# Two transformer blocks in float32 on one core: first loads and gains from ScalarE's queue, another order of the opening products, zeros before two products

## The chip, the core and the metric

The kernel runs on one core of one Trainium2 chip. The metric is device time in microseconds (us) of one execution, and the median of several executions is taken. Before the change it is 1272.45 us, the median of 3 runs (1271.78 to 1274.7).

## The reference

The input x has 256 rows of 1024 columns, float32. Two layers run one after the other, each with three parts, and a last norm follows:

```python
for l in range(2):
    x = x + 0.5 * swiglu(rms_norm(x, ffn1_norm[l]), ffn1_w_gate[l], ffn1_w_up[l], ffn1_w_down[l])
    x = x + hybrid_mixer(rms_norm(x, mix_norm[l]), w_in[l], ...)
    x = x + 0.5 * swiglu(rms_norm(x, ffn2_norm[l]), ffn2_w_gate[l], ffn2_w_up[l], ffn2_w_down[l])
return rms_norm(x, final_norm)
```

`swiglu` multiplies by a gate and an up matrix of 1024 x 2816, forms silu(gate) * up, and multiplies by a down matrix of 2816 x 1024. `hybrid_mixer` has three kinds of attention, gates and an output matrix. All weights are float32, 247 MB are moved in all, and each weight is used once in an execution.

## The kernel before

**Products in three parts.** Each operand is split into a high and a low part. ScalarE writes the high part (`high`, L185), VectorE subtracts it to get the low part (`low`, L188), and TensorE adds up three matmuls (`mm3`, L176 to L178): high by high, low by high, high by low. So each piece of weights goes through four hands before TensorE can use it: a DMA into a raw place, ScalarE, VectorE, TensorE.

**Order.** The kernel writes out the instruction order of three engines itself: `ORDERED` (L61) names TensorE, ScalarE and VectorE, and they issue what they are given in the order in which the Python code emits it, DMA triggers on ScalarE included. SyncE (SP) and GpSimd (POOL) are ordered by a scheduler, which may put a load far ahead of its place in the program. The Python code keeps a clock of its own (`spend`, `defer`, `need`): `defer(us, fn)` emits work when TensorE's planned time has come that far.

**Loads.** `plan` and `plan_product` list the jobs in the order of use. `load` (L313) issues the DMA of a job, and emits the first step of its split at once and the others later. For a job without additions that first step is ScalarE's `high` of the whole job. The high and low parts lie in a ring of 6656 columns, so the splits run some jobs ahead of TensorE.

**A feed forward.** `first_block` (L574) multiplies two row tiles (t = 0, 1) by the first 256 columns of gate, then of up, k = 0 to 7 each. Two single blocks follow (`block`, g2 and u2). Then two units of seven products each for gate (G) and for up (U) come in the order 1, 5, 6, 3, 7, 2, 4, a Strassen scheme that needs sums of weight quarters: `steps` (L277) says for each product which quarter is loaded into which raw place (a with two buffers, b, c and d with one) and what is added by VectorE (L351) or by a POOL DMA (L331). Between the products stand blocks and down products: G1, D0, G5, g3, G6, u3, G3, D1, G7, D2, G2, g4, G4, u4, U1 and so on. So the raw places are filled for the first time by the loads for G1 (a), G5 (b), G6 (c), G2 (d) and U1 (the other a), each 768 KB, from L322.

**Norms.** `norm` (L405) makes one of these chains for the next part: square on ScalarE, root on VectorE and POOL, scale on VectorE (L450, L452), eight transposes on TensorE (`turn`), split (`parts_of`). The gains come by `gain_tile` (L208) on SP. The first norm has its gain by columns: `parts_of` multiplies (L471) and then splits. The opening (L1177 to L1196) loads x and the first weights, issues nine matmuls of zeros (L1186) and runs this norm for the first row tile; `second` (L1198) starts the second one, and `opened` (L1207) loads the tables `rot` and `tab` that the mixers use.

Of the kernel before, what the change touches and what calls it, by code (L numbers as in the profile page):

```python
# [13 lines left out]
ALU = mybir.AluOpType  # L14
AX = mybir.AxisListType

P = 128
# [93 lines left out]
def block_kernel(ctx: ExitStack, tc: tile.TileContext, a: dict, c: dict, out: bass.AP):  # L111
# [57 lines left out]
    def transpose(o, src, n=P):  # L169
        nc.tensor.transpose(o, src, ident[:n, :n])  # L170
        spend(0.11)

    def mm3(o, st, mv, first, last, again=False):

        (sh, sl), (mh, ml) = st, mv
        nc.tensor.matmul(o, sh, mh, start=first, stop=False, skip_group_check=again)  # L176
        nc.tensor.matmul(o, sl, mh, start=False, stop=False, skip_group_check=again)  # L177
        nc.tensor.matmul(o, sh, ml, start=False, stop=last, skip_group_check=again)  # L178
        spend(3 * (max(256, o.shape[-1]) / 2400 + 0.003))
        load_some()  # L180
        while later and later[0][0] <= clock[0]:
            heapq.heappop(later)[2]()
# [25 lines left out]
    def gain_tile(src, n, name, tag):  # L208

        g = small.tile([P, n], F32, tag=tag, name=name, bufs=1)  # L210
        nc.sync.dma_start(g, bass.AP(tensor=src.tensor, offset=src.offset, ap=[[0, P], [1, n]]))
        return g

    def x_in(t):
# [98 lines left out]
    def load(j, ring):  # L313
        job = jobs[j]
        name, n = job["name"], job["n"]
        adds = []
        if "unit" in job:
            places, new, add, source, more = job["unit"]
            if new:
                tag, src = new  # L320
                places[tag] = raw_place("raw" + tag, unit_pool[0], 2 if tag == "a" else 1, [P, 4 * UC], f"{name}_r", j)
                nc.sync.dma_start(places[tag][0].rearrange("p (k n) -> p k n", k=4), src)  # L322
            for t in {source, *(add or ()), *(more or ())[:1]}:
                for i in places[t][1]:
                    if i in loaded:
                        loaded[i][2]()
                if places[t][1][-1] != j:
                    places[t][1].append(j)
            if more:
                tag, src = more  # L330
                nc.gpsimd.dma_start(places[tag][0].rearrange("p (k n) -> p k n", k=4), src, accum_op=ALU.add)  # L331
            raw = places[source][0]
            if add:
                to, other = [places[t][0] for t in add]
                adds = [(to, other)]
        else:
            o, old = take(raws, n, j)
            for i in old:
                loaded[i][2]()
            raw = raws["tile"][:, o:o + n]  # L340
            o = 0
            for w, k0, k1, c0, m in job["runs"]:
                e = o + (k1 - k0) * m
                nc.sync.dma_start(raw[:, o:e].rearrange("p (k n) -> p k n", k=k1 - k0),
                                  w[k0 * P:k1 * P, c0:c0 + m].rearrange("(k p) n -> p k n", p=P))
                o = e
        o, _ = take(rings[ring], n, j)
        hi, lo = [rings[ring][i][:, o:o + n] for i in ("hi", "lo")]
        piece = n // 2 if adds else n if job["whole"] else PIECE
        cuts = [(o, min(n, o + piece)) for o in range(0, n, piece)]  # L350
        todo = [lambda o=o, e=e: nc.vector.tensor_tensor(to[:, o:e], to[:, o:e], other[:, o:e], op=ALU.add)  # L351
                for to, other in adds for o, e in cuts]
        todo += [lambda o=o, e=e: high(hi[:, o:e], raw[:, o:e]) for o, e in cuts]
        todo += [lambda o=o, e=e: low(lo[:, o:e], raw[:, o:e], hi[:, o:e]) for o, e in cuts]
        total = len(todo)

        def until(m):
            while len(todo) > m:
                todo.pop(0)()

        size = piece / 1200 + 0.1
        for m in range(total - 1, -1, -1):
            defer(size * (total - 1 - m), lambda m=m: until(m))
        until(total - 1)
        loaded[j] = hi, lo, lambda: until(0), ring
        return SUM if adds else SPLIT if "unit" in job else PACE * n
# [35 lines left out]
        tl = const.tile([P, KT, S], F32R, tag="xTl", name=f"{name}_Tl")  # L402
        return th, tl

    def norm(name, gain_src, last=None, gain_cols=None):  # L405


        st = {}

        def half_done(t, h):  # L410
            if "g" not in st:
                g = gain_cols is None and gain_tile(gain_src, D, f"{name}_g", "gain")
                st["g"] = g and [g[:, half_cols(i)] for i in range(2)]
                if last is None:
                    nT[name] = transposed(name)
            if h == 0:
                if last is not None:
                    st["xg", t] = row_tile(f"{name}_xg{t}")
                if last is not None and t == 0:
                    st["sq"] = row_tile(f"{name}_sq")  # L420
                st[t] = st["sq"] if last is not None else row_tile(f"{name}_xs{t}"), small.tile([P, 2], F32, tag="ss", name=f"{name}_ss{t}"), \
                    small.tile([P, 1], F32, tag="rstd", name=f"{name}_r{t}")
            defer(0.7, lambda: square(t, h))
            if last is not None:
                nc.vector.tensor_tensor(st["xg", t][:, half_cols(h)], x[t][:, half_cols(h)], st["g"][h], op=ALU.mult)
# [13 lines left out]
        def scaled(t):  # L439
# [8 lines left out]
            for h in range(2):  # L448
                if gain_cols is not None:
                    nc.vector.tensor_scalar(xs[:, half_cols(h)], x[t][:, half_cols(h)], r, None, op0=ALU.mult)  # L450
                else:
                    nc.vector.scalar_tensor_tensor(xs[:, half_cols(h)], x[t][:, half_cols(h)], r, st["g"][h], op0=ALU.mult, op1=ALU.mult)  # L452
                defer(0.8 + 0.7 * h, lambda h=h: turn(t, h))
            made.add((name, t, "rows"))

        def turn(t, h):
            tp = tp_bank(f"{name}_tp{t}{h}")
            for k in range(4):
                kk = h * 4 + k
                transpose(tp[:, k, :], st[t][0][:, kk * P:(kk + 1) * P])  # L460
            defer(0.3, lambda: parts_of(t, h, tp))

        def parts_of(t, h, tp):
            th, tl = nT[name]
            src = tp
            if name[0] == "f":
                if h == 0:
                    kept[name, t] = row_tile(f"{name}_xr{t}").rearrange("p (k s) -> p k s", s=P)
                if gain_cols is not None:
                    src = kept[name, t][:, h * 4:h * 4 + 4, :]  # L470
                    nc.vector.tensor_tensor(src, tp, gain_cols[:, h * 4:h * 4 + 4, None].to_broadcast([P, 4, P]), op=ALU.mult)  # L471
                    made.add((name, "kept", t, h))
            split(th[:, h * 4:h * 4 + 4, rows(t)], tl[:, h * 4:h * 4 + 4, rows(t)], src)
            if name[0] == "f" and gain_cols is None:
                defer(1.5, lambda: (nc.scalar.activation(kept[name, t][:, h * 4:h * 4 + 4, :], tp, AF.Copy), made.add((name, "kept", t, h))))
            made.add((name, t, h))
            if t == 1 and h == 1:
# [53 lines left out]
    def ffn(name, done, opening=None, opened=None):  # L531
        xTh, xTl = nT[name]
        steps, tail, f_first = ffn_steps()
        with ExitStack() as ctx2:
# [24 lines left out]
            def glu(g, u, nm, then, key):  # L559
# [11 lines left out]

                defer(0.25, silu)

            def first_block():  # L574

                pair = hidden(0, 2)
                for t in range(NT):
                    ab = acc_bank(f"{name}_b0{t}").rearrange("p (a b) -> p a b", a=2)
                    for i in range(2):
                        for k in range(KT):  # L580
                            need((name, t, k // 4))
                            mm3(ab[:, i, :], (xTh[:, k, rows(t)], xTl[:, k, rows(t)]), part(f"{name}_{'gu'[i]}0", k),
                                k == 0, k == KT - 1)
                        if opening and t == 0 and i == 0:
# [10 lines left out]
                                            made.update((name, "hT", i, t) for i in range(2))))  # L595

                    glu(ab[:, 0, :], ab[:, 1, :], f"{name}_b0{t}", lambda h, t=t: defer(2.5, lambda: turn(t, h)), (name, "h", 0, t))
                if opening:
                    opened()

            single = {}

# [120 lines left out]

            first_block()
            for step in steps:
                if step[0] == "P":
                    unit_product(*step[1:])
                elif step[0] == "B":
# [452 lines left out]
    nc.scalar.dma_start(gain_rows, a["ffn1_norm"][0].rearrange("(k p) -> k p", p=P))  # L1181
    nc.scalar.dma_start(ident, c["eye"])
    table(AF.Square)
    heat = acc_bank("heat")
    for _ in range(WARM):
        nc.tensor.matmul(heat[:, :256], zeros[:, :P], zeros, start=True, stop=True)  # L1186
    gain_bank = tp_bank("gain_tp")
    transpose(gain_bank[:, 0, :KT], gain_rows, KT)
    gain_cols = small.tile([P, KT], F32, tag="gc", name="gain_cols", bufs=1)
# [2 lines left out]
    first(0, 0)  # L1192
    first(0, 1)
    need(("f1_0", 0, "rows"))
    load(queues[0].pop(0), 0)
    need(("f1_0", 0, 0), ("f1_0", 0, 1))  # L1196

    def second():  # L1198
        x_in(1)
# [5 lines left out]
        pace[0] = clock[0]  # L1205

    def opened():  # L1207
        nc.sync.dma_start(rot, c["rot"])
        nc.sync.dma_start(tab, c["tab"])

    def write(t, h, rows_):
        (nc.scalar, nc.sync)[h].dma_start(out[0, rows(t), half_cols(h)], rows_[:, half_cols(h)])
# [2 lines left out]
    for i, (kind, l) in enumerate(layers):  # L1215
        if i + 1 < len(layers):
            k2, l2 = layers[i + 1]
            done = norm(f"{k2}_{l2}", a[norms[k2]][l2])
        else:
            done = norm("last", a["final_norm"], last=write)  # L1220
        if kind == "mx":
# [35 lines left out]
```

## Time and profile before

| | us |
|---|---|
| median of 3 runs | 1272.45 |
| the profiled execution's own time | 1275.12 |
| its span, first to last instruction | 1273.3 |
| TensorE busy in the span | 1254.1 |
| VectorE busy | 913.9 |
| ScalarE busy | 748.1 |

The profiled execution lies 2.67 us above the median. Times in the rows are counted from the start of the span. In a row of a timeline, the two numbers are the start and the duration in us, then come engine, line, operation, output<-inputs, shapes; in brackets stands how long the engine had been idle and what it waited for. PE is TensorE, DVE VectorE, ACT ScalarE; SPq and ACTq are DMA triggers.

### The profile page before, as it was taken

Reading aid. Unit: us, or ns where it says so; the run is one execution under the profiler, and the core shown is the slowest. Engines: PE = TensorE matmul, PEld = TensorE weight load, DVE = VectorE, ACT = ScalarE, POOL = GpSimd, SP = SyncE. Lnnn points to the kernel's source line nnn. Section 1 sums busy time; section 2 is a strip of 40 time slices with the busy share of each in tenths; the row PEclk is TensorE's granted clock in tenths of the full one; section 3 lists DMA queues with packets and bytes.
Section 4 is the critical chain, followed back from the end, with each engine's and each line's share of the span. In section 5 each row is a group of like instructions: output and inputs, shape, how many; then the busy total and the mean of one; then the engine's idle time right before and its main releaser. Section 6 shows DMA issues by size and latency. Waiting matters only on the chain.

```text
span 1273.3 us, 21204 instructions
## 1 busy us (share of the span) xinstructions
PE 1254.1 (98%) x8287; PEld 1178.7 (93%) x8287; DVE 913.9 (72%) x1359; ACT 748.1 (59%) x1263; POOL 55.6 (4%) x54
## 2 busy tenths in 40 slices
PE   7999999999999999999999999999999999999997
PEld 6999988999999899999889999899999998999996
DVE  5988767765546868887688877667655577788774
ACT  5665646655556456665466565467655554665652
POOL 0000001000000000000000000000000000000000
PEclk8999999999999999999999999999999999999999
DMA  9997856545435688986589985565464466799762
GB/s 301 259 263 207 225 189 172 153 131 145 127 111 169 208 256 221 267 229 174 165 261 261 247 239 151 168 178 154 134 165 115 135 198 199 215 267 242 221 167 79
DMA packets 206308, 247.28 MB, mean 194 GB/s; under 512 B 7160, under 2 KB 190208, under 8 KB 206208
## 3 DMA queue, kind: packets, MB, share of 16 engines
q1 hardware_dynamic: 188864, 220.16, 56.1%
q0 software_dynamic: 16896, 25.17, 12.1%
q8 instruction: 65, 1.06, 0.3%
q10 hardware_dynamic: 448, 0.59, 0.1%
q14 instruction: 35, 0.29, 0.1%
HBM read 244.85 MB, written 1.05 MB: 193 GB/s over the span
## 4 chain that ended last, share of the span: by engine, by line
PE 94%; DVE 3%; ACT 1%; DMA 1%; issue 0%; POOL 0%; POOLq 0%; ACTq 0%; DVEq 0%
PE f_a L178 6%; PE f_a L177 6%; PE f_a L176 6%; PE f_s L176 6%; PE f_s L177 6%; PE f_s L178 6%; PE f_b L177 6%; PE f_b L178 6%; PE f_b L176 6%; PE mx_ogate L176 4%; PE mx_ogate L178 3%; PE mx_ogate L177 3%; PE mx_odqk L176 2%; PE mx_odqk L177 2%; PE mx_odqk L178 2%; PE mx_sbdil L846 1%
## 5 line engine op out<-in xcount | busy, mean ns | idle before, releaser
L188 DVE TENSOR_TENSOR w_l<-w_r,w_h 128x512 fp32r<-128x512 f32 (+1 forms) x484 | 386.4, 824 | 96.7 <-ACT w_h L185 95.0
L185 ACT ACTIVATE w_h<-w_r 128x512 fp32r<-128x512 f32 (+1 forms) x484 | 344.3, 734 | 96.6 <-PE f_a L177 16.8
L176 PE MATMUL f_b<-f_Th,w_h 128*128 128x256 f32 x512 | 144.8, 283 | 0.0
L177 PE MATMUL f_b<-f_Th,w_l 128*128 128x256 f32 x512 | 144.6, 282 | 0.0
L178 PE MATMUL f_b<-f_Tl,w_h 128*128 128x256 f32 x512 | 144.6, 282 | 0.0
L178 PE MATMUL f_a<-w_l,f_hTh 128*128 128x512 f32 x352 | 139.8, 397 | 0.0
L176 PE MATMUL f_a<-w_h,f_hTh 128*128 128x512 f32 x352 | 139.1, 395 | 0.0
L177 PE MATMUL f_a<-w_h,f_hTl 128*128 128x512 f32 x352 | 138.7, 394 | 0.0
L188 DVE TENSOR_TENSOR w_l<-f_U_r,w_h 128x1536 fp32r<-128x1536 f32 (+1 forms) x72 | 100.2, 1399 | 33.1 <-ACT w_h L185 31.9
L185 ACT ACTIVATE w_h<-f_G_r 128x1536 fp32r<-128x1536 f32 (+1 forms) x72 | 86.2, 1199 | 46.4 <-DVE f_G_r L351 18.6
L176 PE MATMUL mx_ogate<-mx_Th,w_h 128*128 128x256 f32 x384 | 113.2, 295 | 0.0
L185 ACT ACTIVATE w_h<-f_U_r 128x1536 fp32r<-128x1536 f32 (+1 forms) x72 | 85.7, 1197 | 41.4 <-issue 14.1
L177 PE MATMUL mx_ogate<-mx_Th,w_l 128*128 128x256 f32 x384 | 108.7, 283 | 0.6 <-DVE w_l L188 0.6
L178 PE MATMUL mx_ogate<-mx_Tl,w_h 128*128 128x256 f32 x384 | 108.6, 283 | 0.0
L188 DVE TENSOR_TENSOR w_l<-f_G_r,w_h 128x1536 fp32r<-128x1536 f32 (+1 forms) x72 | 100.0, 1398 | 10.6 <-ACT w_h L185 10.2
L178 PEld LDWEIGHTS f_b<-f_Tl,w_h 128*128 128x128 f32 x512 | 97.9, 191 | 0.0
L177 PEld LDWEIGHTS f_b<-f_Th,w_l 128*128 128x128 f32 x512 | 97.7, 191 | 0.0
L176 PEld LDWEIGHTS f_b<-f_Th,w_h 128*128 128x128 f32 x512 | 97.6, 191 | 0.0
L176 PE MATMUL f_s<-w_h,f_Sh 128*128 128x384 f32 x256 | 87.3, 341 | 0.0
L178 PE MATMUL f_s<-w_l,f_Sh 128*128 128x384 f32 x256 | 86.7, 339 | 0.0
L177 PE MATMUL f_s<-w_h,f_Sl 128*128 128x384 f32 x256 | 86.6, 338 | 0.0
L178 PEld LDWEIGHTS f_a<-w_l,f_hTh 128*128 128x128 f32 x352 | 66.1, 188 | 15.7
(269 smaller groups left out, 2937.3 us busy)
## 6 DMA issues: line engine op xcount, KB each, us to landing
w_r<-in_ffn_w_down SPq DMA_DIRECT2D x88, 512.0 KB, 4.4
w_r<-in_w_in SPq DMA_DIRECT2D x84, 512.0 KB, 3.9
f_G_r<-in_ffn_w_gate SPq DMA_DIRECT2D x32, 768.0 KB, 7.7
f_U_r<-in_ffn_w_up SPq DMA_DIRECT2D x32, 768.0 KB, 8.6
w_r<-in_ffn_w_gate SPq DMA_DIRECT2D x40, 512.0 KB, 6.1
w_r<-in_ffn_w_up SPq DMA_DIRECT2D x40, 512.0 KB, 6.3
f_G_r<-in_ffn_w_gate POOLq DMA_DIRECT2D x16, 768.0 KB, 8.8
f_U_r<-in_ffn_w_up POOLq DMA_DIRECT2D x16, 768.0 KB, 8.4
```

The source lines that it names most:

```text
L176: nc.tensor.matmul(o, sh, mh, start=first, stop=False, skip_group_check=again)
L177: nc.tensor.matmul(o, sl, mh, start=False, stop=False, skip_group_check=again)
L178: nc.tensor.matmul(o, sh, ml, start=False, stop=last, skip_group_check=again)
L185: nc.scalar.activation(hi, src, AF.Copy)
L188: nc.vector.tensor_tensor(lo, src, hi.bitcast(F32), op=ALU.subtract)
L846: nc.tensor.matmul(o if len(k.shape) == 2 else o.rearrange("p (a b) -> p a b", a=NT), q, k, start=True, stop=True)
```

## The change

- `warm(n)` issues n matmuls of zeros. It is used with 9 at the start as before, with 3 ahead of the first product, and with 5 ahead of the second row tile's transposes in the norm that follows a second feed forward (that is between the two layers).
- Gains, `rot` and `tab` are loaded from ScalarE's queue. A norm's gain is emitted 40 planned us after the norm was set up, and `opened` is called before G4 of the first unit instead of after the first block.
- The first load into each raw place of the units (five loads in all) is issued from ScalarE's queue, the others from SP's as before.
- In the first norm, the multiplications by the gain and ScalarE's high parts come first, VectorE's low parts 1.2 planned us later; the second half's transposes follow 0.1 instead of 0.7 after the first's; the first weights' split is emitted 0.9 later.
- The first row tile's gate products go in two groups of four k: the four high by high, then the four low by high, then the four high by low (`by_parts`).

```diff
+    def warm(n):
+        heat = s_bank("heat")
+        for _ in range(n):
+            nc.tensor.matmul(heat[:, :256], zeros[:, :P], zeros, start=True, stop=True)
...
     def gain_tile(src, n, name, tag):
...
-        nc.sync.dma_start(g, bass.AP(tensor=src.tensor, offset=src.offset, ap=[[0, P], [1, n]]))
+        nc.scalar.dma_start(g, bass.AP(tensor=src.tensor, offset=src.offset, ap=[[0, P], [1, n]]))
...
                 places[tag] = raw_place("raw" + tag, unit_pool[0], 2 if tag == "a" else 1, [P, 4 * UC], f"{name}_r", j)
-                nc.sync.dma_start(places[tag][0].rearrange("p (k n) -> p k n", k=4), src)
+                first = len(users["raw" + tag]) <= (2 if tag == "a" else 1)
+                (nc.scalar if first else nc.sync).dma_start(places[tag][0].rearrange("p (k n) -> p k n", k=4), src)
...
-    def norm(name, gain_src, last=None, gain_cols=None):
+    def norm(name, gain_src, last=None, gain_cols=None, warmed=False):
...
+        if gain_cols is None:
+            defer(40.0, fetch)
...
-                defer(0.8 + 0.7 * h, lambda h=h: turn(t, h))
+                defer(0.8 + (0.7 if gain_cols is None else 0.1) * h, lambda h=h: turn(t, h))
...
         def turn(t, h):
+            if warmed and t == 1 and h == 0:
+                warm(5)
...
+            if gain_cols is not None:
+                src = kept[name, t][:, h * 4:h * 4 + 4, :]
+                nc.vector.tensor_tensor(src, tp, gain_cols[:, h * 4:h * 4 + 4, None].to_broadcast([P, 4, P]), op=ALU.mult)
+                made.add((name, "kept", t, h))
+                high(hi, src)
+                defer(1.2, lambda: (low(lo, src, hi), made.add((name, t, h))))
+                if t == 1 and h == 1:
+                    table(AF.Silu)
+                return
...
+            def by_parts(o, t, k0):
+                ks = range(k0, k0 + 4)
+                w = [part(f"{name}_g0", k) for k in ks]
+                for i, (a, b) in enumerate(((xTh, 0), (xTl, 0), (xTh, 1))):
+                    for k in ks:
+                        nc.tensor.matmul(o, a[:, k, rows(t)], w[k - k0][b], start=k == 0 and i == 0, stop=k == KT - 1 and i == 2)
+                spend(4 * 0.33)
...
+                            if opening and t == 0 and i == 0:
+                                if k % 4 == 0:
+                                    by_parts(ab[:, i, :], t, k)
+                                continue
...
-                if opening:
-                    opened()
...
+                if opening and step == ("P", 0, "G", 4):
+                    opened()
...
-    load(queues[0].pop(0), 0)
+    defer(0.9, lambda: load(queues[0].pop(0), 0))
     need(("f1_0", 0, 0), ("f1_0", 0, 1))
+    warm(3)
...
-        nc.sync.dma_start(rot, c["rot"])
-        nc.sync.dma_start(tab, c["tab"])
+        nc.scalar.dma_start(rot, c["rot"])
+        nc.scalar.dma_start(tab, c["tab"])
...
-            done = norm(f"{k2}_{l2}", a[norms[k2]][l2])
+            done = norm(f"{k2}_{l2}", a[norms[k2]][l2], warmed=kind == "f2")
```

## Rows read from the trace of the kernel before

**Rows 1.** The page, busy us (share of the span) x instructions.
```profile
PE 1254.1 (98%) x8287; PEld 1178.7 (93%) x8287; DVE 913.9 (72%) x1359; ACT 748.1 (59%) x1263; POOL 55.6 (4%) x54
```
**Rows 2.** Waits of TensorE in the whole span: us in total, times, longest.
```profile
PE f_tp L170 <- DVE f_xs L452: 1.8, 1, 1.8
...
PE mx_tp L170 <- DVE mx_xs L452: 0.8, 2, 0.4
```
**Rows 3.** Windows: length; busy us of PE, PEld, DVE, ACT, POOL; granted clock, DMA.
```profile
11.90:18.70 6.80, 5.71 (x24) 5.14 (x25) 5.43 (x11) 4.46 (x10) 0.55 (x1) 0.50 1.01 346
25.50:28.95 3.45, 3.40 (x16) 3.40 (x17) 2.75 (x5) 2.61 (x5) 0.00 (x0) 0.51 1.09 358
28.59:43.70 15.11, 15.11 (x111) 14.60 (x111) 15.03 (x22) 8.64 (x13) 1.45 (x1) 0.99 1.00 298
650.18:653.60 3.42, 3.42 (x19) 3.42 (x18) 2.43 (x3) 1.29 (x3) 0.00 (x0) 0.50 1.12 342
```
**Rows 4.** Timeline of the DMA triggers on SP in the opening.
```profile
6.50 1.35 SPq L322 DMA_DIRECT2D f_G_r<-in_ffn_w_gate  x1
...
14.95 0.38 SPq L344 DMA_DIRECT2D w_r<-in_ffn_w_gate  x1
```
**Rows 5.** Timeline of ScalarE in the first feed forward.
```profile
20.59 1.58 ACT L185 ACTIVATE w_h<-w_r 128x1024 fp32r<-128x1024 f32 x2 [3.23 <-DMA w_r<-in_ffn_w_gate]
...
29.32 1.49 ACT L185 ACTIVATE w_h<-f_G_r 128x1536 fp32r<-128x1536 f32 x1 [0.76 <-ACT f_f_b_s L564]
30.74 1.06 ACT L185 ACTIVATE w_h<-w_r 128x1024 fp32r<-128x1024 f32 x1
...
40.13 0.37 ACT L564 ACTIVATE f_f_b_s<-f_b 128x256 f32<-128x256 f32 x1
...
54.00 0.39 ACT L564 ACTIVATE f_f_b_s<-f_b 128x256 f32<-128x256 f32 x1 [1.30 <-PE f_b L178]
...
59.84 1.49 ACT L185 ACTIVATE w_h<-f_G_r 128x1536 fp32r<-128x1536 f32 x1 [1.81 <-issue]
```
**Rows 6.** Timeline of VectorE in the first feed forward.
```profile
13.57 0.69 DVE L188 TENSOR_TENSOR f_Tl<-f_xr,f_Th 128x512 fp32r<-128x512 f32 x1 [0.70 <-ACT f_Th L185]
14.18 1.89 DVE L188 TENSOR_TENSOR w_l<-w_r,w_h 128x512 fp32r<-128x512 f32 x3
...
30.98 1.75 DVE L188 TENSOR_TENSOR w_l<-f_G_r,w_h 128x1536 fp32r<-128x1536 f32 x1
...
34.72 0.95 DVE L351 TENSOR_TENSOR f_G_r<-f_G_r,f_G_r 128x768 f32<-128x768 f32 x1
...
42.40 0.95 DVE L351 TENSOR_TENSOR f_G_r<-f_G_r,f_G_r 128x768 f32<-128x768 f32 x1
...
45.38 1.95 DVE L188 TENSOR_TENSOR w_l<-f_G_r,w_h 128x768 fp32r<-128x768 f32 x2
...
56.70 1.76 DVE L188 TENSOR_TENSOR w_l<-f_G_r,w_h 128x1536 fp32r<-128x1536 f32 x1
...
65.16 1.76 DVE L188 TENSOR_TENSOR w_l<-f_U_r,w_h 128x1536 fp32r<-128x1536 f32 x1 [0.77 <-ACT w_h L185]
```
**Rows 7.** Timeline of TensorE: starts of the second row tile, G6, G2, U1.
```profile
24.83 0.38 PE L176 MATMUL f_b<-w_h,f_Th 128*128 128x256 f32 x1 [0.53 <-ACT f_Th L185]
...
48.81 0.34 PE L176 MATMUL f_s<-w_h,f_Sh 128*128 128x384 f32 x1
...
63.62 0.34 PE L176 MATMUL f_s<-w_h,f_Th 128*128 128x384 f32 x1
...
73.55 0.34 PE L176 MATMUL f_s<-w_h,f_Th 128*128 128x384 f32 x1
```
**Rows 8.** DMA issues (KB each, us to landing): one alone at 460.66; the fifth of five at 462.98.
```profile
f_G_r<-in_ffn_w_gate SPq DMA_DIRECT2D x1, 768.0 KB, 4.5
...
f_U_r<-in_ffn_w_up SPq DMA_DIRECT2D x1, 768.0 KB, 10.6
```
**Rows 9.** TensorE by groups between 5.1 and 7.2 us: busy, mean ns.
```profile
L1186 PE MATMUL heat<-zeros 128*128 128x256 f32 x10 | 2.5, 393 | 0.0
```

More of the change, by code (lines that the diff above doesn't have):

```diff
@@ L403, in transposed, with fetch @@
         return th, tl
-    def norm(name, gain_src, last=None, gain_cols=None):
+    def norm(name, gain_src, last=None, gain_cols=None, warmed=False):
         st = {}
+        def fetch():
+            if "g" not in st:
+                g = gain_tile(gain_src, D, f"{name}_g", "gain")
+                st["g"] = [g[:, half_cols(i)] for i in range(2)]
+        if gain_cols is None:
+            defer(40.0, fetch)
         def half_done(t, h):
-            if "g" not in st:
-                g = gain_cols is None and gain_tile(gain_src, D, f"{name}_g", "gain")
-                st["g"] = g and [g[:, half_cols(i)] for i in range(2)]
+            if "begun" not in st:
+                st["begun"] = True
+                if gain_cols is None:
+                    fetch()
                 if last is None:
@@ L464, in parts_of @@
             th, tl = nT[name]
-            src = tp
-            if name[0] == "f":
[L467 to L474, printed above, removed]
+            hi, lo = [o[:, h * 4:h * 4 + 4, rows(t)] for o in (th, tl)]
+            if name[0] == "f" and h == 0:
+                kept[name, t] = row_tile(f"{name}_xr{t}").rearrange("p (k s) -> p k s", s=P)
+            if gain_cols is not None:
[7 more added lines that the diff above has]
+                return
+            split(hi, lo, tp)
+            if name[0] == "f":
                 defer(1.5, lambda: (nc.scalar.activation(kept[name, t][:, h * 4:h * 4 + 4, :], tp, AF.Copy), made.add((name, "kept", t, h))))
@@ L1183, in block_kernel @@
     table(AF.Square)
-    heat = acc_bank("heat")
-    for _ in range(WARM):
-        nc.tensor.matmul(heat[:, :256], zeros[:, :P], zeros, start=True, stop=True)
+    warm(WARM)
     gain_bank = tp_bank("gain_tp")
```

## The prediction

> **What bounds the kernel now.** The page's busy times come first: TensorE works through 98% of the span, the other engines through 72% and less [rows 1], so the kernel is bound by TensorE, and a change can only win where TensorE stands still or runs at its lower clock. The list of TensorE's waits says where that is: nearly everything lies in the first 26 us, one gap of 1.8 us lies between the two layers, and two gaps of 0.4 us lie at the mixers' starts [rows 2]. [...] From 28.59 to 43.7 us VectorE is busy for 15.03 of 15.11 us while TensorE never waits [rows 3]: the splits of the first unit's weights are only just ahead of their use. G6's low part is made in two pieces from 45.38 on, the first done by 46.35 (half of 1.95 us), and TensorE begins G6 at 48.81 [rows 6, 7]: a lead of 2.45 us. It is the smallest lead of the unit; G2 has 63.62 - 58.46 = 5.2 us and U1 73.55 - 66.92 = 6.6 us [rows 6, 7].
>
> **The opening.** TensorE reaches the second row tile at 24.83 [rows 7]. Following the chain back: ScalarE stood for 3.23 us at the weights of g2, which landed just before 20.59 [rows 5], because SP could issue them only at 14.95 [rows 4], when VectorE had finished the low part of the first weights and so cleared their raw place [rows 6]. In that low part's queue VectorE waited 0.70 us for ScalarE, and so it did once more before it [rows 6]. With the new order (both gain products, then the low parts) the six VectorE steps of 0.6 to 0.7 us follow each other without those two waits, and the place is clear near 13.5: 1.4 us earlier. G1's 768 KB and the tables no longer stand on SP ahead of g2 [rows 4]; without them I take 4.5 us for landing instead of 5.6 [rows 8]. So g2 lands near 17.9, 2.7 us earlier, and the chain behind it (high parts, low parts, the second tile's gain products) comes along: second tile at 22.1. The bounds of this are 1.4 (the DMA is no quicker) and 4.4 us (the half clock of 25.5 to 28.95, worth 3.45 / 2 = 1.7, goes too).
>
> The products by parts and the three zeros have no term of their own: TensorE finishes the first tile's products sooner, but then waits for g2's chain. Nine zeros stay as they were. Three matmuls of zeros are six passes of 0.21 us and lie in the wait for the first high part.
>
> **The five loads.** This is the term that decides. In the before, SP issued G1's load at 6.50 [rows 4], 23 us before ScalarE used it at 29.32 without waiting for data [rows 5]. On ScalarE's queue the trigger stands in the written order, and `load` emits the high part directly behind the DMA. So ScalarE triggers, and waits for the landing, with all that is queued behind it: the next weights' high parts, silu, the splits of hidden values; VectorE then waits for ScalarE. What a landing costs, L, is bounded by two rows: a load of this size alone took 4.5 us, the fifth of five issued within 2.3 us took 10.6 [rows 8], which is 4.5 plus some 2.1 for each one ahead less the time between the issues. I take 4.5, since SP runs dry while the splits stand still.
>
> [...]
>
> Step by step, times in the trace's own span:
> - G1: ScalarE is free at 29.32 - 0.76 = 28.56 in the before [rows 5]; less 2.7, and 0.4 for the low parts that now follow, 25.5. Landing at 30.0, high part to 31.5 (1.49), so VectorE's low part starts at 31.5 instead of 30.98 [rows 6]: +0.5, though TensorE is 2.7 earlier. G1 itself is not late.
> - G5: VectorE adds the quarter from raw place b at 34.72 [rows 6]. Its trigger stands behind G1's high part, D0's (1.06), a split and a silu (0.37 each) [rows 5]: 33.3, landing 37.8. +3.1.
> - G6: in the before its trigger's place is behind the silu at 40.13 to 40.50 [rows 5], 5.8 us after G5's addition: 37.8 + 5.8 = 43.6, landing 48.1 instead of an addition at 42.40 [rows 6]. +5.7. Less the lead of 2.45, TensorE begins G6 **3.2 us later** than before. The whole gain of the opening is used up on the way: VectorE sets this time.
> - G2: VectorE recovers 1 of ScalarE's 1.3 us of idle time at 54.00 [rows 5] (5.7 - 1.0 = 4.7 behind), then 4.5 for the landing: 9.2 behind, less the lead 5.2 and the 3.2 that TensorE has lost: **+0.8**.
> - U1: 9.2 behind, less 1.8 idle at 59.84 [rows 5] and 1.1 at shorter waits, plus 0.9 for the triggers of `rot` and `tab` (0.38 each at best [rows 4]), plus 4.5: 11.7, less the lead 6.6 and the 4.0 lost: **+1.1**.
>
> Sum of the first feed forward: +5.1. Every us of L counts five times (three at G6, one each at G2 and U1). From U5 on the loads are SP's again and run ahead as before.
>
> **Zeros between the layers.** TensorE's gap ends with the norm's scale, so zeros cannot shorten it. Five matmuls are ten passes; ten took 2.5 us at the opening's full clock with the ends of the first and last counted [rows 9], some 2.1 back to back, 0.3 more than the gap [rows 2]. If the clock stays up, the 3.42 us at half clock behind it, in which TensorE never waited [rows 3], give back 1.7. **-1.4**, between +0.3 (the clock falls anyway) and -1.7.
>
> **Gains from ScalarE.** q_norm's and kv_norm's triggers stand at each mixer's start, just ahead of the squares on which the waits of 0.4 us hang [rows 2]. Two triggers of 0.4 to 0.5 us, less the idle time in which they fall: +0.3 each, **+0.6**; bounds 0 and 2. The norms' gains are emitted in mid-stage, where ScalarE has idle time (59% busy [rows 1]); uncovered they would cost 0.4 us each.
>
> **Sum:** +5.1 - 1.4 + 0.6 = +4.3. Against the profiled execution, 1275.12 + 4.3 = 1279.4; that execution stands 2.67 above the median, so in medians 1272.45 + 4.3 = **1276.7 us**. Some 0.2% (2.5 us) is what a measurement of this kernel can tell from no change.
>
> **Rivals.**
> - *The loads are covered* (faster). If ScalarE's five triggers stand far enough ahead of their use, or land within 3.4 us, G6's lead holds, and the opening's 2.7, with part of the 1.7 of the clock, reaches the end: -3.3 - 1.4 + 0.6 = -4.1, **1268.3**. It decides at 3L = 10.2, or L = 3.4: below that TensorE meets G6 no later than before. For it: a scheduler put SP's G1 load 23 us ahead [rows 4, 5]. Against it: ScalarE is one of the three engines whose order is written out, and a load of this size took 4.5 us with nothing ahead of it [rows 8]. [...]
> - *Partly covered.* With L at 3.8 in effect (ScalarE somewhat earlier at its triggers than I put it), 5 x 0.7 = 3.5 us less: 1276.7 - 3.5 = **1273.2**, not to be told from no change.
> - *Shared bandwidth.* SP's loads of g3, u3 and D1 are in flight beside ScalarE's; L = 5.5: +5.0, **1281.7**.
> - *Zeros do nothing*: the clock falls between the layers all the same, +1.7: **1278.4**. This would be the part of the change that does not do what it is said to.
>
> **How the numbers follow.** The serial landings, with the last two rivals as their variants, 0.55: slower. Covered, 0.25: faster. Partly covered, 0.20: same. The forecast's own range is 1274 to 1282; the other cases pull the lower end to the covered case's 1268.3, the upper end to L of nearly 6: 1268 to 1283.
>
> **What would show it.** Right: ScalarE idles over 3 us before L185 on f_G_r, released by a DMA that it triggered itself just before; VectorE idles before L351; TensorE waits, where it never did, before G6 near 50 us, and may show a lower clock behind it; the second row tile starts near 22; no window of half clock after 650. Wrong: landings of ScalarE's loads that end before their high part is due, TensorE busy without a break from 30 to 75 us, or a first feed forward that ends earlier than before.

## The result, and the profile after

The changed kernel takes 1289.42 us (median of 4 runs, 1287.93 to 1292.18) against 1273.56 us of the kernel before in the same series: ratio 1.0131, 95% interval 1.0118 to 1.0144. It is 15.9 us slower. The prediction had the sign and the reason, but 1276.7 us and a range that ended at 1283. The profiled execution took 1288.44 us, its span is 1286.7 us.

The longest of TensorE's waits in the whole span (us in total, times, longest), in answer to [rows 2]:

```profile
PE f_s L182 <- ACT w_h L191: 4.1, 1, 4.1
PE f_b0tp L170 <- DVE f_f_b_h L590: 3.9, 1, 3.9
PE f_s L182 <- DVE f_G_g L717: 2.5, 1, 2.5
```

All three are new: ahead of G2, ahead of the transposes of the second row tile's first hidden values, and ahead of U1. The wait of 1.8 us between the layers is gone; a stretch of zeros stands there.

TensorE's timeline at the start of the second row tile and of G6, and where it waited, in answer to [rows 7]:

```profile
21.50 0.38 PE L182 MATMUL f_b<-w_h,f_Th 128*128 128x256 f32 x1 [0.52 <-ACT f_Th L191]
...
36.89 0.69 PE L170 MATMUL f_b0tp<-ident,f_f_b_h 128*128 128x128 f32 x2 [3.88 <-DVE f_f_b_h L590]
...
51.53 0.34 PE L182 MATMUL f_s<-w_h,f_Sh 128*128 128x384 f32 x1
...
70.58 0.69 PE L182 MATMUL f_s<-w_h,f_Th 128*128 128x384 f32 x1 [4.08 <-ACT w_h L191]
...
86.52 0.49 PE L182 MATMUL f_s<-w_h,f_Th 128*128 128x384 f32 x1 [2.48 <-DVE f_G_g L717]
```

Against [rows 7] the second tile starts 3.3 us earlier (24.83 to 21.50), G6 2.7 us later (48.81 to 51.53), G2 7.0 us later (63.62 to 70.58) and U1 13.0 us later (73.55 to 86.52). From there to the end little is added, since 1.7 us of half clock behind U1 and 1.4 us gained between the layers nearly cancel: the spans differ by 13.4 us. All of the loss lies between 21 and 90 us.

ScalarE's timeline shows the cause, in answer to [rows 5] (a row with ACTq is a DMA trigger):

```profile
21.43 0.39 ACTq L329 DMA_DIRECT2D f_G_r<-in_ffn_w_gate  x1
...
24.42 0.36 ACT L586 ACTIVATE f_f_b_s<-f_b 128x256 f32<-128x256 f32 x1
29.68 1.49 ACT L191 ACTIVATE w_h<-f_G_r 128x1536 fp32r<-128x1536 f32 x1 [4.90 <-DMA f_G_r<-in_ffn_w_gate]
29.88 0.39 ACTq L329 DMA_DIRECT2D f_G_r<-in_ffn_w_gate  x1
31.08 1.04 ACT L191 ACTIVATE w_h<-w_r 128x1024 fp32r<-128x1024 f32 x1
32.02 0.36 ACT L191 ACTIVATE f_hTh<-f_b0tp 128x256 fp32r<-128x256 f32 x1
32.29 0.38 ACT L586 ACTIVATE f_f_b_s<-f_b 128x256 f32<-128x256 f32 x1
...
59.59 0.38 ACTq L329 DMA_DIRECT2D f_G_r<-in_ffn_w_gate  x1
69.05 1.48 ACT L191 ACTIVATE w_h<-f_G_r 128x1536 fp32r<-128x1536 f32 x1 [9.04 <-DMA f_G_r<-in_ffn_w_gate]
...
73.96 0.37 ACTq L329 DMA_DIRECT2D f_U_r<-in_ffn_w_up  x1
...
82.64 1.48 ACT L191 ACTIVATE w_h<-f_U_r 128x1536 fp32r<-128x1536 f32 x1 [8.01 <-DMA f_U_r<-in_ffn_w_up]
```

ScalarE stands 4.9, 9.04 and 8.01 us at loads that it triggered itself just before, those of G1, G2 and U1. Behind G1's high part stand D0's (31.08), the split of the first tile's hidden values (32.02) and silu of the second tile (32.29). VectorE stands the same way, behind ScalarE at G1, at G6's quarter, and behind ScalarE at G2 and U1:

```profile
31.20 1.76 DVE L194 TENSOR_TENSOR w_l<-f_G_r,w_h 128x1536 fp32r<-128x1536 f32 x1 [3.04 <-ACT w_h L191]
...
34.95 0.95 DVE L358 TENSOR_TENSOR f_G_r<-f_G_r,f_G_r 128x768 f32<-128x768 f32 x1
...
36.42 0.41 DVE L590 TENSOR_TENSOR f_f_b_h<-f_f_b_s,f_b 128x256 f32<-128x256 f32 x1
...
47.22 0.96 DVE L358 TENSOR_TENSOR f_G_r<-f_G_r,f_G_r 128x768 f32<-128x768 f32 x1 [4.51 <-DMA f_G_r<-in_ffn_w_gate]
...
70.56 1.76 DVE L194 TENSOR_TENSOR w_l<-f_G_r,w_h 128x1536 fp32r<-128x1536 f32 x1 [9.63 <-ACT w_h L191]
...
84.16 1.76 DVE L194 TENSOR_TENSOR w_l<-f_U_r,w_h 128x1536 fp32r<-128x1536 f32 x1 [7.43 <-ACT w_h L191]
```

The hidden values of the second tile (36.42) are what TensorE waits 3.88 us for at 36.89. Their silu had ended at 32.67; what held them was VectorE, which works without a break from G1's low part at 31.20 on. In the kernel before they came at nearly the same time, but TensorE came for them only at 37.66, 1.06 us after they were done:

```profile
36.19 0.41 DVE L568 TENSOR_TENSOR f_f_b_h<-f_f_b_s,f_b 128x256 f32<-128x256 f32 x1
```

```profile
37.66 0.38 PE L170 MATMUL f_b0tp<-ident,f_f_b_h 128*128 128x128 f32 x2
```

The landings of the five loads, from the list of DMA issues (KB each, us from trigger to landing), in the order G1, G5, G6, G2, U1:

```profile
f_G_r<-in_ffn_w_gate ACTq DMA_DIRECT2D x1, 768.0 KB, 8.1
...
f_G_r<-in_ffn_w_gate ACTq DMA_DIRECT2D x1, 768.0 KB, 4.5
...
f_G_r<-in_ffn_w_gate ACTq DMA_DIRECT2D x1, 768.0 KB, 7.5
...
f_G_r<-in_ffn_w_gate ACTq DMA_DIRECT2D x1, 768.0 KB, 9.4
...
f_U_r<-in_ffn_w_up ACTq DMA_DIRECT2D x1, 768.0 KB, 8.6
```

Only G5's takes the 4.5 us of a load alone [rows 8]. Last, the windows at half clock, in answer to [rows 3]:

```profile
35.51:42.33 6.82, 5.44 (x21) 5.44 (x22) 6.82 (x11) 3.89 (x7) 1.45 (x1) 0.50 0.38 100
...
69.64:76.47 6.83, 5.10 (x16) 4.60 (x17) 5.91 (x5) 4.99 (x6) 0.00 (x0) 0.50 0.58 162
86.71:90.12 3.41, 3.41 (x12) 3.41 (x12) 3.29 (x4) 1.85 (x4) 0.28 (x1) 0.50 0.64 198
```

Each lies behind or around one of the new waits; none is left in the opening or between the layers. TensorE works 13.95 us in them, which by the granted clock of 0.50 costs at most half, an estimate of 7.0 us; in the profile of before it was 5.71 + 3.40 + 3.42, half of it 6.3 us. There 128x256 matmuls start every 0.21 us at 0.50 (652.0 on) and every 0.12 at 1.00 (653.8 on). So the clock has moved to other places and is no large part of the difference by itself.

### The profile page after: what moved, and what is told of

It reads as the page before. It is cut to its first block, busy times and chain, and to the rows that moved or that the text cites. A ratio compares the mean times of both kernels' runs of the same rounds, so it can differ in the third digit from the quotient of the medians.

```text
span 1286.7 us, 21240 instructions
## 1 busy us (share of the span) xinstructions
PE 1259.0 (98%) x8303; PEld 1182.1 (92%) x8303; DVE 913.1 (71%) x1359; ACT 746.8 (58%) x1263; POOL 55.6 (4%) x54
## 3 DMA queue, kind: packets, MB, share of 16 engines
q1 hardware_dynamic: 184496, 211.71, 53.4%
q8 instruction: 65, 1.06, 0.3%
## 4 chain that ended last, share of the span: by engine, by line
PE 91%; DVE 3%; DMA 3%; ACT 1%; issue 1%; POOL 0%; POOLq 0%; ACTq 0%; DVEq 0%
PE f_a L184 6%; PE f_a L183 6%; PE f_a L182 6%; PE f_s L182 6%; PE f_s L183 6%; PE f_s L184 6%; PE f_b L182 5%; PE f_b L183 5%; PE f_b L184 5%; PE mx_ogate L182 4%; PE mx_ogate L183 4%; PE mx_ogate L184 4%; DMA f_G_r<-in_ffn_w_gate 2%; PE mx_odqk L182 2%; PE mx_odqk L183 2%; PE mx_odqk L184 2%
```

## The experiments

**The five loads back on SP (e1_sp).** One line of the changed kernel:

```diff
-                first = len(users["raw" + tag]) <= (2 if tag == "a" else 1)
+                first = False
```

> The changed kernel with the five first loads (G1, G5, G6, G2, U1) back on SP's queue and nothing else undone. Theory: the five loads carry the whole loss, the opening gains 4.8 us (first tile stage ends at 26.88 instead of 31.69) and the zeros between the layers 1.0, and these reach the end once TensorE no longer waits for the units: about 1267.8 us, 5 to 6 under the kernel before, no wait of TensorE over 1 us between 30 and 90 us. Rival: the moved table and gain triggers or the new order of the opening cost as well: the time stays above 1276.

Measured: 1272.84 us, ratio to before 0.9999 (0.9990 to 1.0008). The whole loss is gone, so it was the five loads'; but none of the expected gain is there either. The first two of them now start on SP ahead of g2, and ScalarE's next step shows it:

```profile
6.43 2.96 SPq L329 DMA_DIRECT2D f_G_r<-in_ffn_w_gate  x2
13.20 0.37 SPq L351 DMA_DIRECT2D w_r<-in_ffn_w_gate  x1
...
20.26 1.57 ACT L191 ACTIVATE w_h<-w_r 128x1024 fp32r<-128x1024 f32 x2 [4.22 <-DMA w_r<-in_ffn_w_gate]
```

g2's load, triggered at 13.20, takes 7.0 us (5.6 in the kernel before, 3.9 in the changed one). What the new order gains at the trigger (14.95 to 13.20) the landing gives back, and the second row tile starts at 24.49. So the opening's gain needs an emptier queue ahead of g2 (7.0 us behind two unit loads, 3.9 behind none), which the same move had bought.

**The five loads alone (e2_only).** The kernel before with the lines on `first` and nothing else.

> The kernel before with the five first loads on ScalarE's queue and nothing else. Theory: the loss is theirs alone, and without the earlier opening TensorE loses about as much: 14 to 19 us over the kernel before (1287 to 1292), waits before G2 and U1, the half clock behind them. Rival: the loss comes from the loads together with the new order of the opening (a wait that falls where the first tile ends 4.8 us earlier): at most 5 us over the kernel before.

Measured: 1289.33 us, ratio 1.0134 (1.0108 to 1.0159), 16.4 us over before. TensorE waits 6.6 us at the second tile's first hidden values, 4.0 ahead of G2 and 2.7 ahead of U1. The rest of the change neither makes the loss nor softens it beyond the noise. This run also has no unit load ahead of g2, but the old order of the opening. g2's load is triggered at 15.21 and takes 4.2 us; the second row tile starts between before (24.83) and after (21.50):

```profile
23.63 0.38 PE L176 MATMUL f_b<-w_h,f_Th 128*128 128x256 f32 x1 [0.52 <-ACT f_Th L185]
```

So the new order alone (e1_sp) brings 0.3 us there, the emptier queue alone 1.2, both together 3.3. The starts of these runs differ by up to 0.4 us.

**Which loads cost how much (e6_gu).** G2's and U1's first loads on SP, the other three on ScalarE:

```diff
-                first = len(users["raw" + tag]) <= (2 if tag == "a" else 1)
+                first = len(users["raw" + tag]) <= 1 and tag != "d"
```

> The changed kernel with G2's and U1's first loads on SP, and G1's, G5's and G6's left on ScalarE. Theory: of the 15.9 us, G2 and U1 with the half clock behind their two waits carry most (TensorE falls from +2.6 to +14.6 us between 48 and 90 us): 1276 to 1279. Rival: the delay already stands in ScalarE's and VectorE's queues when G6 has been split and G2 would be late whoever loads it: 1284 or more.

Measured: 1279.38 us, ratio 1.0049 (1.0035 to 1.0064), just above the theory's span and far below the rival's. Against the changed kernel some 10 us are G2's and U1's; against e1_sp 6.5 us are left for G1, G5 and G6.

**The same queue, triggered early (e3_early).** All five triggers on ScalarE's queue, but together behind u2's high part.

```diff
+        if name.startswith("f1_0_u2"):
+            fetch_units()
```

> The changed kernel with the same five loads on the same queue, ScalarE's, but all five triggers emitted together right behind the high part of u2, ahead of the first silu. Theory: the place of the trigger, right ahead of its own high part, is what costs; the queue itself does not: about 1268 us (5 to 6 under the kernel before), G2's and U1's landing long before their high parts. Rival: ScalarE's queue is served badly beside SP's and POOL's, wherever the trigger stands: over 1280, ScalarE still waiting for G2's or U1's load.

Measured: 1273.74 us, ratio 1.0009 (1.0000 to 1.0018): 15.7 us better than in the written places, so the place of the trigger is what costs. But it is not the expected 1268. ScalarE's timeline:

```profile
22.14 0.95 ACTq L325 DMA_DIRECT2D f_G_r<-in_ffn_w_gate  x2
...
26.40 3.65 ACTq L325 DMA_DIRECT2D f_U_r<-in_ffn_w_up  x1
30.09 0.38 ACT L598 ACTIVATE f_f_b_s<-f_b 128x256 f32<-128x256 f32 x1 [4.87 <-issue]
```

The five triggers take 7.9 us from the first to the end of the last (22.14 to 30.05), the last alone 3.65, and silu of the first tile stands behind them for 4.87 us. The wait has only changed its name: ScalarE now stands at issuing instead of at the landing, and TensorE waits 3.2 us behind it, with 6.8 us at half clock around the wait (a mean granted clock of 0.66 from 30 to 40 us).

**One load ahead of g2, none in ScalarE's order (e12_one).** All five on SP, but VectorE writes one column of four of the places late in its order, so that only G1's load can start ahead of g2:

```diff
+    def gate():
+        for tag in "bcd":
+            gated[tag] = raw_place("raw" + tag, unit_pool[0], 1, [P, 4 * UC], f"gated_{tag}", None)
+            nc.vector.tensor_copy(gated[tag][0][:, :1], x[1][:, :1])
...
+                places[tag] = gated.pop(tag) if tag in gated else raw_place(...)
...
+                first = False
...
+                if tag == "a" and len(users["rawa"]) == 1:
+                    gated[tag] = raw_place("rawa", unit_pool[0], 2, [P, 4 * UC], "gated_a", None)
+                    nc.vector.tensor_copy(gated[tag][0][:, :1], x[1][:, :1])
...
+        if name.startswith("f1_0_u2"):
+            gate()
```

> The changed kernel with all five first loads on SP, but only G1's may start ahead of g2: one column of each of the other four places is written by VectorE (four copies of 128x1) at the point where the high part of u2, and for U1 that of G1, stands in VectorE's order, so their loads wait for it. Theory: in the kernel before and in the kernel with the five loads back on SP, two transfers stand ahead of g2 on SP and its landing takes 5.6 and 7.0 us; in the changed kernel none do and it takes 3.9. With one ahead it takes about 4, the first tile stage ends near 27 to 28, no load stands in ScalarE's order, and the opening's gain of 4 and the 1.0 between the layers reach the end: 1267 to 1269 us. Rival: the transfers only fit into the first 40 us one way or another, and what g2 gains G5's or G6's quarter loses: no faster than 1271.

Measured: 1270.48 us (1269.78 to 1270.84), ratio 0.9983 (0.9974 to 0.9991): faster than both kernels, by 2.0 us where 3.5 to 5.5 were expected. The 1.0 us expected of the zeros is not there (below); why the rest is not there stays open. g2's load takes 3.8 us, and none of the three new waits is left but 0.8 us:

```profile
34.56 0.44 PE L170 MATMUL f_b0tp<-ident,f_f_b_h 128*128 128x128 f32 x2 [0.80 <-DVE f_f_b_h L603]
```

Ahead of 1266 us the granted clock never falls in this profile (1.00 from 6.5 to 1266). TensorE reaches the second tile's transposes at 34.56, 2.3 us ahead of the changed kernel in spite of a start that was 0.8 us later in this run.

**G1's load alone on ScalarE (e13_g1act).** As e12_one, with `first = tag == "a" and len(users["rawa"]) == 1`.

> The kernel of e12_one with G1's load alone on ScalarE's queue, in the written place of the changed kernel, right ahead of G1's own high part. Theory: ScalarE stands at G1's landing (5 us in the changed kernel) and D0's high part, hidden values and silu of the second tile stand behind it, so TensorE waits near 4 us for the first block's hidden values of the second tile: 3 to 5 us over e12_one, 1270 to 1273. Rival: G1's landing is covered as the prediction had it (+0.5 at VectorE, nothing at TensorE): within 1 us of e12_one.

Measured: 1278.02 us, ratio 1.0042 (1.0028 to 1.0056), 7.5 us over e12_one. G1's cost is real, and larger than expected. SP now issues two unit loads within 0.5 us of G1's trigger:

```profile
21.70 0.46 ACTq L337 DMA_DIRECT2D f_G_r<-in_ffn_w_gate  x1
...
33.22 1.48 ACT L191 ACTIVATE w_h<-f_G_r 128x1536 fp32r<-128x1536 f32 x1 [8.17 <-DMA f_G_r<-in_ffn_w_gate]
...
PE f_b0tp L170 <- DVE f_f_b_h L603: 7.1, 1, 7.1
```

The same trigger at almost the same time takes 11.5 us (21.70 to 33.22) instead of 8.1, and TensorE's wait grows from 3.9 to 7.1 us. SP's queue moved 1.07 MB in the 3.8 us behind the trigger, against 0.85 MB in 3.6 us in the changed kernel; which of SP's loads count for how much is not shown, for in e2_only G1's load took 10.0 us with no unit load on SP.

**G2's load alone on ScalarE (e14_g2act).** As e12_one, with `first = tag == "d" and len(users["rawd"]) == 1`.

> The kernel of e12_one (no load in ScalarE's order, 1270.5 us) with G2's load alone on ScalarE's queue, right ahead of its own high part. The lead of G2's split over TensorE is 5.2 us in the kernel before. Theory: SP has up to five loads of its own in flight there, and the landing takes 9 to 9.5 us as in the changed kernel, so TensorE waits some 4 us ahead of G2 or U1 and the clock falls behind it: 4 to 6 us over e12_one, 1274.5 to 1276.5. Rival (the prediction's size): SP's queue is dry, the landing takes 4.5 us, the lead covers it: within 1 us of e12_one.

Measured: 1278.03 us, ratio 1.0038 (1.0025 to 1.0051), by the ratios 7.0 us over e12_one. The prediction's size (covered by the lead) is refuted; the theory's 4 to 6 us were still too small:

```profile
gated_d<-in_ffn_w_gate ACTq DMA_DIRECT2D x1, 768.0 KB, 9.2
...
PE f_s L182 <- ACT w_h L191: 2.8, 1, 2.8
...
PE f_s L184 <- DVE w_l L194: 1.2, 1, 1.2
...
64.61:71.44 6.83, 5.99 (x23) 5.99 (x24) 6.83 (x7) 5.41 (x6) 0.00 (x0) 0.50 0.77 219
```

2.8 + 1.2 us of waiting, and half of 5.99 us at half clock, make 7.0. One load of 768 KB in the wrong place of the order costs over three times what e12_one gains (2.0 us).

**Without the products by parts and the three zeros (e5_noparts).** The changed kernel less these two edits.

> The changed kernel without the products by parts and without the three matmuls of zeros ahead of the first product; all else as changed. Theory (the prediction's: no term of their own, since TensorE waits for g2's chain in any case): within 2 us of the changed kernel, 1287.5 to 1291.5. Rival: they carry a part of the 4.8 us by which the first tile stage ends earlier, by the clock: the stage ends over 1 us later than 26.9, and half clock shows ahead of 27 us.

Measured: 1287.75 us, ratio 1.0122 (1.0108 to 1.0136), an interval that overlaps that of the changed kernel. The first tile's stage ends at 27.3 us (26.9 in the changed kernel, which started 0.55 earlier). A half clock of 3.4 us does show at 12.7 us (0.50 up to 16.14), as the rival had it, but TensorE then waits 0.23 us (at 17.57) instead of 1.32 (at 17.03) for the next low part, and the second tile starts at 21.94 against 21.50, no later once the 0.55 of the start are taken off. No term of their own shows, as predicted.

**The zeros between the layers alone (e4_zeros).** The kernel before with `warm(5)` there.

> The kernel before with five matmuls of zeros ahead of the second row tile's transposes between the two layers, and nothing else. Theory: the clock does not fall after 650 us: 1.0 to 1.7 us less, 1271.2 to 1272.0. Rival: the zeros delay the transposes by as much as the clock gives back: within 0.5 us of the kernel before.

Measured: 1272.60 us, ratio 1.0007 (0.9998 to 1.0015): no gain. **The best kernel without them (e16_nozeros):**

> The kernel of e12_one without the five matmuls of zeros between the layers. Theory: without them the clock falls after 645 us as in the profile of before, which costs 1.0 to 1.7 us: 1271.5 to 1272.2, granted clock lower by 0.001 to 0.002. Rival (after the kernel before with the zeros alone showed no gain): a typical run has no half clock between the layers, and the zeros change nothing: within 0.5 us of e12_one.

Measured: 1270.70 us, ratio 0.9978 (0.9970 to 0.9987), the same as with them. In its profile the clock stays full although the wait of 1.8 us is back in its place, which leaves TensorE busy for 8.17 of these 10 us:

```profile
645.00:655.00 10.00, 8.17 (x70) 8.18 (x70) 8.78 (x12) 5.68 (x10) 0.92 (x1) 1.00 1.10 353
```

**The kernel before, profiled twice more (b2 and b3).**

> The kernel before once more, for a second profile. If the two falls of the clock behind 25 and behind 650 us belong to the kernel, both show again and the run takes 1273 to 1275; if they depend on where the clock's steps fall in a run, one or both are missing and the run is 1 to 3 us shorter than the 1275.12 of the first profile.

> The kernel before a third time, for a third profile: as for b2. Two profiles that differ in these windows with the same program settle that they are not the kernel's alone.

Measured: 1273.11 and 1274.85 us. The window around 650 us, first of b2, then of b3:

```profile
650.08:653.50 3.42, 3.42 (x32) 3.42 (x30) 2.77 (x5) 2.49 (x6) 0.00 (x0) 1.00 1.11 340
```

```profile
649.53:652.94 3.41, 3.41 (x18) 3.41 (x18) 2.61 (x4) 1.29 (x3) 0.00 (x0) 0.50 1.11 347
```

The same program, the same wait ahead of it, and the clock falls in one execution and not in the other. The two times differ by 1.74 us, about half of 3.42, though executions of this kernel also differ by more than that. The falls in the opening (from 11 and from 25 us) stand in all three profiles of before, but in e4_zeros, the same kernel up to the zeros, there is one fall from 13.6 us and none near 25.

## Why the prediction was right in kind and wrong in size

**The opening: right.** Predicted: g2's trigger near 13.5, landing 4.5, second tile at 22.1. Measured: 13.36, 3.9, 21.50. Also right was that it is used up on the way. The step's reasons were two, the new order (1.4) and the shorter landing (1.3). Each alone brings less: 0.3 us in e1_sp, where two loads stand ahead of g2, and 1.2 in e2_only with the old order.

**The failed step** is the landing in "The five loads": "I take 4.5, since SP runs dry while the splits stand still." It measured 8.1, 4.5, 7.5, 9.4 and 8.6 us. SP does not run dry at G1, G2 and U1: its queue moved 0.85 MB from 21.43 to 25 us, 0.79 from 59.6 to 63 and 1.21 from 73.96 to 78. At G5 and G6 it all but does (0.01 MB), but beside G6's load POOL's accumulating load is in flight, which the step left out. The packets by queue (packets, MB, share of 16 engines), first for G6's load (39.6 to 47.1), then from G2's trigger at 59.6 to 63.0, then from 63 to its landing at 69 (q1 is SP's queue, q0 POOL's, q10 ScalarE's):

```profile
q0 software_dynamic: 391, 0.60, 45.5%
q10 hardware_dynamic: 528, 0.79, 40.2%
...
q1 hardware_dynamic: 677, 0.79, 68.2%
q0 software_dynamic: 181, 0.25, 42.5%
...
q1 hardware_dynamic: 930, 1.51, 69.3%
q10 hardware_dynamic: 528, 0.79, 36.4%
```

For 3.4 us no packet of G2's load moves while SP and POOL move theirs; then it gets 36.4% of the engines' time beside SP's 69.3%. G1's and U1's start as slowly: 0.01 of 0.79 MB from 21.43 to 25 us and 0.08 from 73.96 to 78. The splits that stand still do not empty SP, because SP runs ahead: between 53.4 and 59.3 it had issued five loads. ScalarE's queue was not the worse served of the two there: SP's own load of 512 KB, issued at 59.25, took 12.1 us. The rival "Shared bandwidth" named this, but with 5.5 us. Why ScalarE's load moves nothing in the first 3.4 us is not shown. For G1, G2 and U1 the other end that the prediction gave, 10.6, was the nearer. The L of nearly 6 at the upper end of the range was the author's estimate and no run listed here shows it: the landings were 4.5 and 7.5 to 9.4 us in the changed kernel, 9.2 to 11.5 in the runs with G1's or G2's load on ScalarE's queue.

**What this did to the sum, by its own steps.** VectorE's low part of G2 was predicted at 56.70 + 9.2 = 65.9 and came at 70.56: 4.7 late, for a landing that was 9.4 - 4.5 = 4.9 longer. U1's was predicted at 65.16 + 11.7 = 76.9 and came at 84.16: 7.3 late, for 4.9 + 4.1 less the slack on the way. TensorE: U1 predicted at 73.55 + 5.1 = 78.65, measured 86.52, 7.9 late. With the half clock behind U1 (3.41 / 2 = 1.7) and the gains from ScalarE at nothing (the waits at the mixers' starts are 0.9 in two, 0.8 before; predicted +0.6), the miss against the profiled execution is 7.9 + 1.7 - 0.6 = 9.0: 1288.44 against the predicted 1279.4.

**Two errors that cancelled.** Up to G6 the numbers look right: TensorE +2.7 (predicted +3.2), VectorE's addition at 47.22 (predicted 48.1). But G1, G5 and G6 were triggered at 21.43, 29.88 and 39.61, some 4 us ahead of the predicted 25.5, 33.3 and 43.6, and G1's and G6's took 3 to 3.6 us longer. G5's predicted +3.1 became +0.2 (34.95 against 34.72 in [rows 6]).

**A wait that it missed.** The prediction let TensorE lose its lead at G6 and said that G1 "itself is not late". G1's low part did come close to the forecast (31.20, predicted 31.5). But the second tile's hidden values stand behind it in VectorE's order, and their lead over TensorE was only 1.06 us in the kernel before, less than the 2.45 of G6. TensorE, free for them at 33.01 (36.89 - 3.88) instead of 37.66, waited there for 3.88 us: that used up all but 0.8 us of the opening's gain. The half clock around this wait (5.44 / 2 = 2.7 us) and 0.7 us of waiting behind G6's quarter made the 2.7 us of delay at G6. e13_g1act shows the price of G1's load alone.

**The zeros between the layers: wrong.** In the profile the step does what was predicted: TensorE is 14.7 us behind the kernel before ahead of the zeros and 13.3 behind them, 1.4 us as predicted. But b2 is an execution of before in which the clock does not fall there, and in the medians the zeros are worth nothing, in e4_zeros and between e12_one and e16_nozeros. The term was taken from one profiled execution as if each had it. This is also a part of why the median lies 12.7 us off, not 9.0: the profiled execution of before lay 2.67 above its median, that of after 0.98 below its own.

**Chances.** The likeliest case had the right sign. The range ended at 1283 because it took L to nearly 6 and not to the row with 10.6.

## What to carry to other kernels

A load moved to the queue of an engine whose order is written out must be triggered a full landing ahead of its use, with the landing taken beside everything that the other queues have in flight (768 KB took 4.5 us with them all but idle, 11.5 in e13_g1act); right ahead of its use, that engine and whoever waits for it stand for it (at G2 ScalarE 9.04 us, VectorE 9.63, TensorE 4.08). Several triggers in a row on that engine are no remedy, since they hold the engine themselves (4.87 us in e3_early); in e12_one SP, which computes nothing in this kernel, did it: 1270.48 us against the changed kernel's 1289.42. Before a gain is credited to a new order, look how much of it hangs on a queue that the same change has emptied and must fill elsewhere. And when one engine is to come earlier, look at every place where it meets another one: the smallest lead there (here 1.06 us), not the one at the next large step, decides what reaches the end.

## What the runs showed of the hardware that was not expected

- In the changed kernel DMA triggers on ScalarE's queue ran ahead of activations that are written in front of them. G5's trigger is written behind D0's high part, the split of hidden values and a silu; it went out at 29.88, and these started at 31.08, 32.02 and 32.29. G1's, written behind u2's high part and a silu, went out at 21.43; the silu started at 24.42. The activations themselves kept their order. What lets a trigger go ahead, no run here tests.
- A trigger's own length is not constant: 0.37 to 0.39 us for the five in the changed kernel, up to 3.65 us as the last of five in a row in e3_early. What is in flight does not set it alone: G2's took 0.38 us at 59.59, with five loads issued on SP in the 6 us before.
- One load of 768 KB from ScalarE's queue took 4.5 us with the other queues all but idle (0.01 MB), 7.5 to 9.4 beside SP's or POOL's loads in the changed kernel, 10.0 as G1's in e2_only, and 11.5 in e13_g1act, where SP issued two unit loads at the same moment.
- Whether the granted clock falls to half behind a wait of 1.8 us differs between executions of one program (1.00 in b2, 0.50 in b3).
